# A low-rank update on one Trainium2 core: TensorE in a hardware loop, x narrowed to float16 before it is turned

## The chip, the core and the metric

The kernel runs on one core of a Trainium2 chip. Times are device microseconds of one execution; the time before is the median of three runs. One further execution was recorded by the hardware profiler, and the views shown here are of that one. Engines are called TensorE (PE; PEld is its weight load, PEldq the queue in front of that), VectorE (DVE), ScalarE (ACT), GpSimd (POOL) and SyncE (SP); a q behind a name is that engine's instruction queue, from which DMAs are issued too.

## What is computed

```python
batch, seq, d_model, r = 16, 512, 768, 16
def reference(x, A, B, scale):        # all float32, scale = 0.5
    lora = np.matmul(np.matmul(x, A), B)
    return (x + scale * lora).astype(np.float32)
```

x is 8192 tokens by 768, 25.2 MB in and as much out. A is 768 x 16 and B 16 x 768. The arithmetic is small; x has to come in, be multiplied twice through a width of 16, be added to the product, and go out.

## The kernel before

The 8192 tokens are 64 subtiles of 128 tokens. They are loaded in six parts of 2, 6, 8, 16, 16 and 16 subtiles (PARTS, line 13), each one DMA, all issued by SyncE (line 68, the last at line 96). All of x stays in SBUF: the result is written over it and stored from there (line 155), by SyncE too, in eight pieces of 2, 6, 8, 16 and then four times 8 subtiles. A and B come in through ScalarE's queue (lines 79, 80) into room that the last part of x takes later, so the last load waits until VectorE has turned and cast them into a_mm and b_mm (lines 87 to 93).

The work goes by chunks of up to four subtiles, 17 in all. For each chunk (the loop at line 157):

- `transposed` (line 109): for each of the six blocks of 128 columns, TensorE turns the chunk's subtiles, in float32, into a bank of PSUM (xt_ps, three buffers; line 113), and ScalarE copies the bank to SBUF as float16 (xt_sb, six buffers; line 115).
- `projected` (line 118): six matmuls with A as weights add up the 16 x 512 projection ps_yt (line 122); VectorE scales it to float16, yt_sb, two buffers (line 127).
- `added` (line 133): for each subtile two matmuls (512 and 256 columns) expand the projection into lora_ps, two buffers (line 139); VectorE adds that to x in place (line 145).
- `finished` (line 147): where a piece is complete, SyncE stores it.

The order on TensorE is written out: three blocks of chunk c turned, half of the previous chunk expanded, three more blocks turned, the other half expanded, then chunk c projected. Every instruction is unrolled. Semaphores are set by the framework from the tiles and their buffers; waits ride on the instruction that needs them.

Of the kernel before, what the change touches and what calls it, by code (L numbers as in the profile page):

```python
# [1 line left out]

# [6 lines left out]


MM_DT = mybir.dt.float16

PARTS = [2, 6, 8, 16, 16, 16]

STORES = {4: [8, 8], 5: [8, 8]}

CHUNK = 4


@with_exitstack  # L20
def kernel(
    ctx: ExitStack,
    tc: tile.TileContext,
    x: bass.AP,
    A: bass.AP,
    B: bass.AP,
    scale: bass.AP,
    out: bass.AP,
):

    nc = tc.nc
    fp32 = mybir.dt.float32
    P = 128

    x2 = x.flatten_outer_dims()
    out2 = out.flatten_outer_dims()
    T, D = x2.shape
    R = A.shape[1]  # L40
    ND = D // P
    assert D % P == 0 and sum(PARTS) * P == T
    n_splits = [(n0, min(512, D - n0)) for n0 in range(0, D, 512)]
    sc = float(scale)

    const = ctx.enter_context(tc.tile_pool(name="const", bufs=1))
    xpool = ctx.enter_context(tc.tile_pool(name="xp", bufs=1))
    xtpool = ctx.enter_context(tc.tile_pool(name="xtp", bufs=6))
    ypool = ctx.enter_context(tc.tile_pool(name="yp", bufs=2))
    ps_xt = ctx.enter_context(tc.tile_pool(name="ps_xt", bufs=3, space=bass.MemoryType.PSUM))  # L50
    ps_y = ctx.enter_context(tc.tile_pool(name="ps_y", bufs=1, space=bass.MemoryType.PSUM))
    ps_l = ctx.enter_context(tc.tile_pool(name="ps_l", bufs=2, space=bass.MemoryType.PSUM))


    parts = []
    tok = 0
    for i, S in enumerate(PARTS):
        parts.append([None, tok, S])
        tok += S * P

    def rows(t2, i):
        _, tok0, S = parts[i]
        return t2[ds(tok0, S * P), :].rearrange("(p s) d -> p s d", s=S)

    def loaded(i):
        S = parts[i][2]
        parts[i][0] = xpool.tile([P, S, D], fp32, name=f"x_sb{i}")
        nc.sync.dma_start(out=parts[i][0], in_=rows(x2, i))  # L68


    last = len(parts) - 1
    lastpool = ctx.enter_context(tc.tile_pool(name="lastp", bufs=1))
    room = lastpool.tile([P, parts[last][2], D], fp32, name="room", tag="last")
    NB = D // 32
    a_rows = room[0:32, 0, 0 : 32 * R].rearrange("b (a r) -> b a r", r=R)
    a_t = room[0:32, 1, 0 : 32 * R].rearrange("a (r b) -> a r b", r=R)
    b_f32 = room[0:R, 2, :]
    nc.gpsimd.memset(a_rows, 0.0)  # L78
    nc.scalar.dma_start(out=a_rows[0:NB, :, :], in_=A.rearrange("(b a) r -> b a r", a=32))
    nc.scalar.dma_start(out=b_f32, in_=B)  # L80
    loaded(0)
    loaded(1)
    for i in range(2, last):
        loaded(i)


    nc.vector.transpose(out=a_t, in_=a_rows.rearrange("b a r -> b r a"))  # L87
    a_mm = const.tile([P, ND, R], MM_DT, name="a_mm")
    a_tv = a_t[:, :, 0:NB].rearrange("a r (c k) -> a k c r", k=4)
    for k in range(4):  # L90
        nc.vector.tensor_copy(out=a_mm[ds(32 * k, 32), :, :], in_=a_tv[:, k, :, :])  # L91
    b_mm = const.tile([R, D], MM_DT, name="b_mm")
    nc.vector.tensor_copy(out=b_mm, in_=b_f32)  # L93

    parts[last][0] = lastpool.tile([P, parts[last][2], D], fp32, name="x_last", tag="last")
    nc.sync.dma_start(out=parts[last][0], in_=rows(x2, last))

    ident = const.tile([P, P], fp32, name="ident")
    make_identity(nc, ident)


    chunks = [
        (i, s0, min(CHUNK, S - s0))
        for i, (_, _, S) in enumerate(parts)
        for s0 in range(0, S, CHUNK)
    ]
    state = {}

    def transposed(c, j):
        i, s0, n = chunks[c]  # L110
        xt_ps = ps_xt.tile([P, CHUNK, P], fp32, name="xt_ps")
        for s in range(n):
            nc.tensor.transpose(xt_ps[:, s, :], parts[i][0][:, s0 + s, ds(j * P, P)], ident)  # L113
        xt_sb = xtpool.tile([P, CHUNK * P], MM_DT, name="xt_sb")
        nc.scalar.copy(out=xt_sb[:, 0 : n * P], in_=xt_ps[:, 0:n, :])  # L115
        state[c, j] = xt_sb

    def projected(c):
        n = chunks[c][2] * P
        ps_yt = ps_y.tile([R, CHUNK * P], fp32, name="ps_yt")  # L120
        for j in range(ND):
            nc.tensor.matmul(  # L122
                ps_yt[:, 0:n], a_mm[:, j, :], state.pop((c, j))[:, 0:n],
                start=(j == 0), stop=(j == ND - 1),
            )
        yt_sb = ypool.tile([R, CHUNK * P], MM_DT, name="yt_sb")
        nc.vector.tensor_scalar(  # L127
            out=yt_sb[:, 0:n], in0=ps_yt[:, 0:n], scalar1=sc, scalar2=None,
            op0=mybir.AluOpType.mult,
        )  # L130
        state[c] = yt_sb

    def added(c, subs):
        i, s0, n = chunks[c]
        subs = [s for s in subs if s < n]
        lora = {s: ps_l.tile([P, D], fp32, name="lora_ps") for s in subs}
        for s in subs:
            for n0, w in n_splits:
                nc.tensor.matmul(  # L139
                    lora[s][:, ds(n0, w)], state[c][:, ds(s * P, P)], b_mm[:, ds(n0, w)],  # L140
                    start=True, stop=True,
                )
        for s in subs:
            xs = parts[i][0][:, s0 + s, :]
            nc.vector.tensor_tensor(out=xs, in0=xs, in1=lora[s], op=mybir.AluOpType.add)  # L145

    def finished(c):
        i, s0, n = chunks[c]
        del state[c]
        end = 0  # L150
        for w in STORES.get(i, [parts[i][2]]):
            end += w
            if end == s0 + n:
                piece = slice(end - w, end)
                nc.sync.dma_start(out=rows(out2, i)[:, piece, :], in_=parts[i][0][:, piece, :])

    for c in range(len(chunks)):
        for j in range(3):
            transposed(c, j)
        if c >= 1:  # L160
            added(c - 1, (0, 1))
        for j in range(3, ND):
            transposed(c, j)
        if c >= 1:
            added(c - 1, (2, 3))
            finished(c - 1)
        projected(c)
    c = len(chunks) - 1
    added(c, (0, 1))
    added(c, (2, 3))  # L170
    finished(c)


# [1 line left out]
_INS = ['x', 'A', 'B', 'scale']  # L175
_OUTS = [((16, 512, 768), 'float32')]

_NUMBERS = {'scale': 0.5}


# [26 lines left out]
```

## Time and profile before

| | |
|---|---|
| time, median of 3 runs | 125.14 us (125.05 to 125.24) |
| the profiled execution | 124.9 us, of which the profile's span is 123.1 us |
| TensorE busy, in 614 matmuls | 97.8 us, 79% of the span |
| TensorE's weight loads | 60.8 us, 49% |
| VectorE busy | 70.3 us, 57% |
| ScalarE busy | 52.5 us, 43% |
| DMA, the queue of SyncE | 50.33 MB, 95.6% of 16 engines' span |
| DMA, instruction fetches (two queues) | 8 packets, 0.10 MB, 0.3% |
| mean rate of all DMA | 410 GB/s |
| chain that ended last | PE 71%, DMA 8%, VectorE 7% |

The span runs from the first instruction of the kernel to its last; the time holds 1.8 us more. A row of the page's groups reads: line, engine, operation, output <- input with shapes, count | busy us, mean ns of one | idle us of the engine just ahead of them and what ended it. A matmul's duration reaches from its start until its result is out, so consecutive ones overlap: their distance is less than the mean of one. The chain of waits follows the work back from the end: each piece started when the one above it was done.

### The profile page before, as it was taken

How to read it: one execution, taken by the hardware profiler on the slowest of the kernel's cores; microseconds unless marked ns; L12 is line 12 of the kernel's file. 1: busy time of each engine (PE TensorE's matmuls, PEld its weight loads, DVE VectorE, ACT ScalarE, POOL GpSimd, SP SyncE). 2: the span in 40 equal slices, each digit the busy share in tenths (PEclk: the TensorE clock that was granted, in tenths of full speed). 3: DMA queues.
4: the chain of work that ended last, by engine and by line, in shares of the span. 5: the costliest groups of instructions: out<-in, count | busy, mean ns of one | idle time of the engine just before them, and what ended most of it. 6: DMA issues, size and time to landing. Idle time of an engine off the chain costs nothing.

```text
span 123.1 us, 1615 instructions
## 1 busy us (share of the span) xinstructions
PE 97.8 (79%) x614; PEld 60.8 (49%) x614; DVE 70.3 (57%) x87; ACT 52.5 (43%) x103; POOL 1.1 (1%) x7
## 2 busy tenths in 40 slices
PE   0095999999949999999999999999999999530000
PEld 0083765657328566656657474757565666100000
DVE  0261056755884276868686868685767768880000
ACT  3060556455406573645555564737373736000000
POOL 3000000000000000000000000000000000000000
PEclk9999999999999999999999999999999999995555
DMA  2999998999799699799799999989979999999981
GB/s 61 406 431 427 471 519 367 415 500 431 335 511 479 290 511 468 319 479 495 295 411 462 444 407 495 479 351 479 452 311 463 415 439 426 421 447 439 415 383 64
DMA packets 2092, 50.54 MB, mean 410 GB/s; under 512 B 252, under 2 KB 252, under 8 KB 548
## 3 DMA queue, kind: packets, MB, share of 16 engines
q1 hardware_dynamic: 2016, 50.33, 95.6%
q10 hardware_dynamic: 68, 0.10, 0.4%
q8 instruction: 5, 0.08, 0.3%
q14 instruction: 3, 0.02, 0.0%
HBM read 25.26 MB, written 25.17 MB: 410 GB/s over the span
## 4 chain that ended last, share of the span: by engine, by line
PE 71%; DMA 8%; DVE 7%; issue 1%; DVEq 1%; SPq 0%; ACT 0%; ACTq 0%
PE xt_ps L113 38%; PE lora_ps L139 18%; PE ps_yt L122 15%; DMA x_sb<-in_x_dram 8%; DVE x_last L145 3%; DVE x_sb L145 3%; DVE yt_sb L127 1%; DVEq L202 1%; SPq L68 0%; ACT xt_sb L115 0%; ACTq L115 0%
## 5 line engine op out<-in xcount | busy, mean ns | idle before, releaser
L115 ACT CAST xt_sb<-xt_ps 128x512 f16<-128x512 f32 (+1 forms) x102 | 51.2, 569 | 49.9 <-PE xt_ps L113 49.6
L145 DVE TENSOR_TENSOR x_sb<-x_sb,lora_ps 128x768 f32<-128x768 f32 x48 | 43.5, 950 | 21.2 <-PE lora_ps L139 21.2
L113 PE MATMUL xt_ps<-ident,x_sb 128*128 128x128 f32 x288 | 39.7, 290 | 7.7 <-DMA x_sb<-in_x_dram 7.6
L113 PEld LDWEIGHTS xt_ps<-ident,x_sb 128*128 128x128 f32 x288 | 33.1, 147 | 16.7 <-issue 11.5
L139 PE MATMUL lora_ps<-b_mm,yt_sb 16*128 16x512 f16 (+1 forms) x128 | 26.8, 324 | 3.8 <-DVE yt_sb L127 1.6
L122 PE MATMUL ps_yt<-xt_sb,a_mm 128*16 128x512 f16 (+1 forms) x102 | 24.4, 375 | 0.0
L145 DVE TENSOR_TENSOR x_last<-x_last,lora_ps 128x768 f32<-128x768 f32 x16 | 14.5, 950 | 5.3 <-PE lora_ps L139 5.3
L139 PEld LDWEIGHTS <-yt_sb 16*128 16x128 f16 x128 | 9.5, 92 | 15.3 <-issue 8.3
L127 DVE TENSOR_SCALAR yt_sb<-ps_yt 16x512 f16<-16x512 f32 (+1 forms) x17 | 10.9, 642 | 7.9 <-PE ps_yt L122 7.9
L122 PEld LDWEIGHTS <-a_mm 128*16 128x16 f16 x102 | 7.9, 91 | 13.0 <-issue 5.1
L113 PE MATMUL xt_ps<-ident,x_last 128*128 128x128 f32 x96 | 12.2, 277 | 0.0
L113 PEld LDWEIGHTS xt_ps<-ident,x_last 128*128 128x128 f32 x96 | 10.3, 140 | 3.0 <-PE ps_yt L122 1.7
L93 DVE CAST b_mm<-room 16x768 f16<-16x768 f32 x1 | 0.5, 548 | 4.4 <-DMA room<-in_B_dram 4.4
L115 ACT ACT_TABLE_LOAD x1 | 1.3, 1283 | 1.9 <-POOL ident masks.py:199 1.9
L87 DVE STREAM_TRANSPOSE room<-room 32x512 f32<-32x512 f32 x1 | 1.0, 1031 | 1.1 <-DMA room<-in_A_dram 1.1
L91 DVE CAST a_mm<-room 32x96 f16<-32x96 f32 x4 | 0.9, 232 | 0.1
L78 POOL MEMSET room<- 32x512 f32 x1 | 0.5, 515 | 0.3 <-POOLq L188 0.3
masks.py:199 POOL TENSOR_SCALAR_AFFINE_SELECT ident<-ident 128x128 f32<-128x128 f32 x1 | 0.3, 292 | 0.1
masks.py:197 POOL MEMSET ident<- 128x128 f32 x1 | 0.2, 194 | 0.0
L188 POOL MEMSET const-bfloat16-1.0<- 128x1 bf16 x1 | 0.1, 101 | 0.0
L188 POOL MEMSET const-uint8-127<- 128x1 uint8 x1 | 0.1, 101 | 0.0
L188 POOL MEMSET const-float32-0.0<- 128x1 f32 x1 | 0.1, 98 | 0.2 <-issue 0.2
(1 smaller groups left out, 0.1 us busy)
## 6 DMA issues: line engine op xcount, KB each, us to landing
x_sb<-in_x_dram SPq DMA_DIRECT2D x2, 6144.0 KB, 39.7
out_dram<-x_sb SPq DMA_DIRECT2D x3, 3072.0 KB, 21.6
x_last<-in_x_dram SPq DMA_DIRECT2D x1, 6144.0 KB, 56.0
out_dram<-x_sb SPq DMA_DIRECT2D x1, 6144.0 KB, 28.2
out_dram<-x_last SPq DMA_DIRECT2D x2, 3072.0 KB, 13.5
x_sb<-in_x_dram SPq DMA_DIRECT2D x1, 3072.0 KB, 17.3
x_sb<-in_x_dram SPq DMA_DIRECT2D x1, 2304.0 KB, 10.5
out_dram<-x_sb SPq DMA_DIRECT2D x1, 2304.0 KB, 44.6
```

The source lines that it names most:

```text
L78: nc.gpsimd.memset(a_rows, 0.0)
L87: nc.vector.transpose(out=a_t, in_=a_rows.rearrange("b a r -> b r a"))
L91: nc.vector.tensor_copy(out=a_mm[ds(32 * k, 32), :, :], in_=a_tv[:, k, :, :])
L93: nc.vector.tensor_copy(out=b_mm, in_=b_f32)
L113: nc.tensor.transpose(xt_ps[:, s, :], parts[i][0][:, s0 + s, ds(j * P, P)], ident)
L115: nc.scalar.copy(out=xt_sb[:, 0 : n * P], in_=xt_ps[:, 0:n, :])
L122: nc.tensor.matmul(ps_yt[:, 0:n], a_mm[:, j, :], state.pop((c, j))[:, 0:n], start=(j == 0), stop=(j == ND - 1),)
L127: nc.vector.tensor_scalar(out=yt_sb[:, 0:n], in0=ps_yt[:, 0:n], scalar1=sc, scalar2=None, op0=mybir.AluOpType.mult,)
L139: nc.tensor.matmul(lora[s][:, ds(n0, w)], state[c][:, ds(s * P, P)], b_mm[:, ds(n0, w)], start=True, stop=True,)
L145: nc.vector.tensor_tensor(out=xs, in0=xs, in1=lora[s], op=mybir.AluOpType.add)
L188: nc = _bacc.Bacc("TRN2", target_bir_lowering=False, num_devices=1)
L202: with _tile.TileContext(nc) as tc:
```

## The change

The kernel body is rewritten with semaphores set by hand; the framework's scheduling of tiles is used for memory only.

- Parts are now 4, 4, 8, 16, 16 and 16 subtiles, stored in pieces of 4, 4, 8, 16 and four times 8. There are 16 chunks of four subtiles.
- x is not turned as float32. It is first narrowed to float16, by pieces of 4 subtiles x 256 columns, into three fixed buffers xh0, xh1 (by VectorE) and xh2 (by ScalarE). TensorE turns these, eight 128 x 128 blocks to a group, into float16 in three PSUM buffers xt_ps0 to 2; ScalarE copies each to xt0 to 2.
- The scaling of the projection goes from VectorE to ScalarE, into one buffer yt. There are two buffers lo_ps for the expanded subtiles, as before.
- A and B are loaded by SyncE, behind the first part of x, and GpSimd makes the identity as float16.
- TensorE runs chunks 1 to 15 as a hardware loop (`nc.Fori`). A loop's instruction can't wait for a rising count, so each of its waits is for one, and takes one off again (`taken`); the unrolled engines wait for rising counts.

The order on each engine is written out:

```diff
+LOADS = [4, 4, 8, 16, 16, 16]
+STORES = [4, 4, 8, 16, 8, 8, 8, 8]
...
+        load(0)
+        nc.sync.wait_ge(S["zeroed"], 1)
+        nc.sync.dma_start(
+            out=a_rows[0:NB, :, :], in_=A.rearrange("(b a) r -> b a r", a=32)
+        ).then_inc(S["a"], 16)
+        nc.sync.dma_start(out=b_f32, in_=B).then_inc(S["b"], 16)
+        for i in range(1, len(LOADS) - 1):
+            load(i)
+        nc.sync.wait_ge(S["prep"], 1)
+        load(len(LOADS) - 1)
...
+        narrowed(nc.scalar, 0, 2)
+        for c in range(NC):
+            for u in range(NU):
+                nc.scalar.wait_ge(S["turned"], NU * c + u + 1)
+                nc.scalar.copy(out=xt[u], in_=xt_ps[u]).then_inc(S[f"got{u}"], 1)
+            if c + 1 < NC:
+                narrowed(nc.scalar, c + 1, 2)
+            nc.scalar.wait_ge(S["proj"], c + 1)
+            nc.scalar.activation(
+                out=yt, in_=yt_ps, func=mybir.ActivationFunctionType.Copy, scale=sc
+            ).then_inc(S["y"], 1)
...
+        def summed(k):
+            nc.vector.wait_ge(S["lora"], k + 1)
+            nc.vector.tensor_tensor(
+                out=xs[:, k, :], in0=xs[:, k, :], in1=lo_ps[k % 2], op=add
+            ).then_inc(S["freed"], 1)
+            if k + 1 in ends:
+                nc.vector.drain().then_inc(S["added"], 1)
...
+        for c in range(NC):
+            for u in range(2):
+                if c + 1 < NC:
+                    nc.vector.wait_ge(S["turned"], NU * c + u + 1)
+                    narrowed(nc.vector, c + 1, u)
+                if c >= 1:
+                    for s in range(2 * u, 2 * u + 2):
+                        summed((c - 1) * CHUNK + s)
+        for s in range(CHUNK):
+            summed((NC - 1) * CHUNK + s)
...
+        def taken(name):
+            nc.tensor.wait_ge(S[name], 1).then_inc(S[name], -1)
+
+        def turned(u):
+            taken(f"fed{u}")
+            for j in range(2):
+                for s in range(CHUNK):
+                    i = nc.tensor.transpose(
+                        xt_ps[u][:, j, ds(s * P, P)], xh[u][:, s, ds(j * P, P)], ident
+                    )
+            i.then_inc(S["turned"], 1)
+
+        def projected(u):
+            taken(f"got{u}")
+            for j in range(2):
+                i = nc.tensor.matmul(
+                    yt_ps, a_mm[:, 2 * u + j, :], xt[u][:, j, :],
+                    start=(u == 0 and j == 0), stop=(u == NU - 1 and j == 1),
+                )
+            if u == NU - 1:
+                i.then_inc(S["proj"], 1)
+
+        def expanded(s):
+            if s == 0:
+                taken("y")
+            taken("freed")
             for n0, w in n_splits:
+                i = nc.tensor.matmul(
+                    lo_ps[s % 2][:, ds(n0, w)], yt[:, ds(s * P, P)], b_mm[:, ds(n0, w)],
                     start=True, stop=True,
                 )
+            i.then_inc(S["lora"], 1)
...
+        with nc.Fori(1, NC, engines=(mybir.EngineType.PE,)):
+            turned(0)
+            expanded(0)
+            expanded(1)
+            turned(1)
+            projected(0)
+            expanded(2)
+            expanded(3)
+            turned(2)
+            projected(1)
+            projected(2)
+        for s in range(CHUNK):
+            expanded(s)
```

In the loop, turned and projected are of chunk c, expanded of chunk c - 1. `narrowed(engine, c, u)` casts columns 256 u to 256 u + 255 of chunk c into xh[u]; each engine waits for a part of x once, at the first chunk of that part. prep is counted up when VectorE has made a_mm and b_mm. SyncE issues the stores in order, each behind a wait for added.

## The prediction

> **What bounds the kernel now.** I read the DMA first, then the chain that ended last, then the rows that price one chunk (four subtiles of 128 tokens). The DMA by stretches (length of the stretch, busy time of five engines with counts, granted clock, mean busy share of the 16 DMA engines, GB/s):
>
> ```profile
> 2.00:64.00 62.00, 54.44 (x337) 34.60 (x338) 35.58 (x46) 30.43 (x61) 0.00 (x0) 1.00 1.00 424
> 64.00:122.00 58.00, 43.34 (x279) 26.22 (x276) 34.73 (x42) 21.89 (x42) 0.00 (x0) 0.90 0.98 418
> ```
>
> The share is 1.00 while x is loaded (the last load lands at 8.2 + 56.0 = 64.2) and 0.98 while the result is stored. All loads and stores go through SP's queue in order, so no store moves before the last load is through. From then on the kernel is a full pipe of stores, as long as each is issued before the one ahead of it is done. The chain of waits nevertheless names TensorE (start us, us, what):
>
> ```profile
> 57.67 1.39 PE ps_yt L122 x6
> 59.06 1.46 PE xt_ps L113 x12
> 60.52 0.75 PE lora_ps L139 x4
> 61.27 1.46 PE xt_ps L113 x12
> 62.73 0.75 PE lora_ps L139 x4
> 63.48 1.39 PE ps_yt L122 x6
> ```
>
> A chunk takes TensorE 1.39 + 2 x 1.46 + 2 x 0.75 = 5.81 us without a gap; the last add ends at 110.4 and the last store is issued at 110.5. So two limits lie almost on each other. By the tile's own view:
>
> ```profile
> DMA to landing us min/median/max: 11.8/15.1/56.0
> ```
>
> The next to last store is issued at 99.9 and lands at 115.0, the last lands at 110.5 + 11.8 = 122.3, 7.3 us behind it. 3.146 MB at 0.43 MB/us are 7.3 us: the queue had no hole. How late could the last issue be? The first load (0.786 MB) took 5.4 us on an empty queue, 1.85 of it transfer at 425 GB/s, so some 3.55 us are fixed; a 3.146 MB store on an empty queue would take 7.4 + 3.55 = 10.95 us. It took 11.8: **slack 0.85 us**, last issue by about 111.35. A faster TensorE can gain next to nothing, since the store pipe is full; a later last add costs its delay, less 0.85 us.
>
> **The change, part by part.** The rows (line, engine, operation, shapes, count, busy us, mean ns, idle before):
>
> ```profile
> L115 ACT CAST xt_sb<-xt_ps 128x512 f16<-128x512 f32 x90 | 47.0, 595 | 44.0 <-PE xt_ps L113 44.0
> L115 ACT CAST xt_sb<-xt_ps 128x256 f16<-128x256 f32 x12 | 4.2, 375 | 5.9 <-PE xt_ps L113 5.6
> L139 PEld LDWEIGHTS <-yt_sb 16*128 16x128 f16 x128 | 9.5, 92 | 15.3 <-issue 8.3 <-DVE yt_sb L127 2.6
> L93 DVE CAST b_mm<-room 16x768 f16<-16x768 f32 x1 | 0.5, 548 | 4.4 <-DMA room<-in_B_dram 4.4
> L113 PEldq EVENT_SEMAPHORE  x4: 51/51/51, 6.1 to 81.0; - x4
> ```
>
> - Loads and stores move the same bytes in the same order; the first 32 subtiles still arrive as four loads, so load 3 should still land at about 2.2 + 32.9 = 35.1. A and B now stand behind load 0 on SP's queue (0.1 MB, 0.2 us). SP's wait for prep before the last load holds only that load and the stores; prep needs some 4 us of VectorE after load 0 lands near 8, so about 12 against the 8.2 of before, with loads queued until 49.6. Nothing lost.
> - Narrowing by VectorE (new, two per chunk, 128x1024): between the b_mm row (768 columns, 548 ns) and the a_mm row (96 columns, 232 ns) a column costs 0.47 ns, so 0.67 us; at the 1 column per 1.04 ns of the 16x512 row from PSUM (673 ns) 1.2 us. I take 0.67, as b_mm is the nearest SBUF row. VectorE per chunk: 2 x 0.67 + 4 x 0.9 = 4.9 us, no bound.
> - ScalarE: three copies 128x1024, one narrowing, one yt. From 256 to 512 columns the row grows by 220 ns, so 1024 columns cost 595 + 440 = 1.03 us. Nothing shows a ScalarE read from SBUF or of float16: 0.6 to 1.5 us, I take 1.03 for both. Back to back it saves 0.1 (six in 3.03 us). ScalarE per chunk 4 x 0.93 + 0.6 = 4.3 us, no bound either.
> - Transposes in float16, eight to a group: float32 ones follow every 121 ns. Float16 projections stream 512 columns in 232 ns, 58 ns for 128 columns, and a float16 weight load has 92 ns against 140. Between 58 and 121 I take 75 ns: 7 x 75 + 235 for the last to come out = 0.76 us. TensorE per chunk: 24 x 0.075 + 1.39 + 1.5 = 4.7 us, plus eleven semaphore instructions of 51 ns, 5.3 us. Below 5.81: by busy time everything gets faster.
> - **The ring of waits** is what I believe decides. lo_ps has two buffers, each waited for by name; yt and the three xh, xt_ps and xt have one each, and TensorE's order is fixed: turned(2) stands behind expanded(3), which needs the first two adds of the previous chunk. Hand-overs cost 0.05 us (VectorE's yt ends 34.34, TensorE starts 34.39). From one copy of xt2 to the next: copy 1.03; narrowing xh2, queued ahead of yt on ScalarE, 0.93; yt 0.50; hand-over and two waits 0.15, expanded(0) 0.48 to its end, hand-over 0.05; two adds 1.82; hand-over, wait and expanded(3) issued 0.05 + 0.05 + 0.375; wait and turned(2) 0.05 + 0.76; hand-over 0.05. **Sum 6.30 us a chunk**, with no engine above 5.3. (Second path to the first add: projection, back edge, turned(0), VectorE's narrowing: about equal.) Low end 5.85 (58 ns transposes, waits free), high end 7.1 (121 ns transposes, 1.5 us narrowing).
>
> The back edge of the loop is nowhere in this trace. The nearest rows are a semaphore instruction, 51 ns, and the smallest load, 3.7 us to landing, should code have to come from memory. I take 0.15 us; about 0.35 us a chunk hides beside ScalarE's narrowing. The Trainium skill (Advanced Engine Details and Errata, Control Flow Timing) gives about 108 ns for compare-and-branch, and its page Runtime: NRT & Kernel Launch, Instruction fetch mechanics, speaks against the change: a taken branch to a target outside the fetched window waits for a DMA. By the first the sum stays; the second would be the third rival; no run here shows either.
>
> **The sum.** VectorE's narrowing for chunk 4 waits for load 3, with chunk 2's adds queued behind it. 35.1 + 0.05 + 0.67 + 1.82 = 37.65; expanded(3), turned(2), copy: + 2.36 = 40.0 (xt2 of chunk 3). Twelve more chunks: + 75.6 = 115.6. Chunk 15: projection 0.70, yt 0.65, expanded 0.63, four adds 3.60 = 121.2; issue 0.15, store on an empty queue 10.95, end 0.8 (122.3 to 123.1 now): span 133.1.
>
> To that the clock. It shows in the same twelve transposes, early and later:
>
> ```profile
> 11.76 2.79 PE L113 MATMUL xt_ps<-ident,x_sb 128*128 128x128 f32 x12 [1.34 <-DMA x_sb<-in_x_dram]
> 15.36 1.53 PE L113 MATMUL xt_ps<-ident,x_sb 128*128 128x128 f32 x12
> ```
>
> Up to 14.8 us TensorE ran at half speed, and at 110.4 the granted clock fell again, after a stretch in which it was busy 1.18 of 3.41 us. With load 3 awaited it will stand still for some 4 us before 37, so a slow stretch behind that is likely: 0 to 3 us, I take 1.0. The Trainium skill (TensorE: Matmul & The Clock Gate, Part 4) says that transposes do not count as activity for the clock; the stretch from 11.76 to 14.8, nearly all transposes, raised it, so here the measurement decides. By the rule the sum would be that of the second rival.
>
> Span 134.1. The profiled execution took 124.9 for its span of 123.1, so + 1.8: **135.9**. (The median of 125.14 is 0.2 above that execution; I leave that out.)
>
> **The rivals.**
> - The ring is shorter: ScalarE and TensorE handle 16-bit data at twice the rate of their float32 rows (copy and narrowing -0.8 together). It decides below (111.35 - 0.15 - 5.58 - 40.0) / 12 = 5.47 us a chunk: then the last store is in time and the pipe of stores ends as now. For it: only float32 sources are in the rows. Against: ScalarE's rate a column is the same in every row. Time: 124.9 less a part of the 0.3% that instruction fetches take now, 124.6.
> - Clock: gaps keep TensorE at half speed. By the two rows above it is then 1.82 times as slow, 4.7 us become 8.6, with the semaphore instructions 9.1 a chunk: 12 x 2.8 more, about 170. Against: stretches busy 2.37 of 3.41 us held the full clock.
> - The back edge fetches code: 3.7 - 0.35 us times 15, up to 186; with a stall of 1 us, 146. Against: the loop's body is some 50 instructions.
>
> **How the numbers follow.** Forecast 0.72, with its own range from 129 (5.85 a chunk: 5.4 less, clock 1 less) to 147 (7.1: 9.6 more, clock 2 more). Shorter ring 0.15, clock 0.08, back edge 0.05. Range 125 to 147: it leaves out most of the shorter ring and the two slow cases' upper part. A measurement tells about 0.2% from no change. Faster 0.11 and same 0.04 are the shorter ring, slower 0.85 the rest.
>
> **What would show it.** Last store issued near 121, DMA share falling below 0.9 after 64 us; chunks 6.3 us apart; TensorE waiting for yt and for VectorE's adds; turned groups of 0.76 us; VectorE's narrowing 0.67, ScalarE's 1.0. Wrong if chunks are under 5.5 us apart, or TensorE's idle time sits at the loop's edge, or the granted clock stays at 0.5.

## The result and the profile after

The changed kernel takes 139.64 us (median of six runs, 137.83 to 141.4) against 125.12 us: **1.110 times as long, 95% interval 1.103 to 1.117**. The prediction was 135.9 us, range 125 to 147. The profiled execution took 141.0 us, its span is 139.2 us. (Ratios and intervals, here and in the experiments, leave out runs more than 1.5% above the fastest of their kernel, here those of 141.0 and 141.4 us, while medians and ranges hold all; why the runs differ so much, TensorE's clock, is a finding below.)

TensorE, granted clock and DMA of the changed kernel, in 40 slices of its span:

```profile
PE   0058509999969699969699999986999998964000
PEclk9999965555899955999955959599959686868555
DMA  4999999999889999989999999999259505950792
```

The clock of the kernel before rose once and stayed at full speed to the end of its work. Here it swings between full and half all the way. The DMA begins to run out of stores after some 70% of the span. By stretches (TensorE, its weight loads, VectorE, ScalarE, GpSimd; clock, DMA share, GB/s):

```profile
2.00:64.00 62.00, 45.10 (x280) 20.22 (x280) 35.67 (x49) 33.36 (x39) 0.12 (x1) 0.81 1.00 422
64.00:122.00 58.00, 52.04 (x319) 21.85 (x318) 40.26 (x50) 37.05 (x42) 0.00 (x0) 0.78 0.82 350
```

Loading is as before: share 1.00. Storing has fallen from 0.98 to 0.82, since the stores are late. The end of VectorE's work, and the stores' times from issue to landing (shortest, median, longest):

```profile
125.58 3.63 DVE L144 TENSOR_TENSOR xs<-xs,lo_ps 128x768 f32<-128x768 f32 x4 [3.40 <-PE lo_ps L202]
```

```profile
DMA to landing us min/median/max: 8.7/15.1/42.9
```

The last add ends at 129.2 instead of 110.4, and the last store, issued at 129.3 and alone in the queue, needs 8.7 us. One chunk at full clock, from one copy of xt2 to the next (start us, us, engine, line, operation):

```profile
59.73 1.01 ACT L133 COPY xt<-xt_ps 128x1024 f16<-128x1024 f16 x1 [1.32 <-PE xt_ps L182]
60.64 1.05 ACT L91 CAST xh<-xs 128x1024 f16<-128x1024 f32 x1
...
60.89 0.59 PE L190 MATMUL yt_ps<-xt,a_mm 128*16 128x512 f16 x2 [0.66 <-PEq L176]
...
61.44 0.61 PE L182 MATMUL xt_ps<-ident,xh 128*128 128x128 f16 x8
61.59 0.58 ACT L137 ACTIVATE yt<-yt_ps 16x512 f16<-16x512 f32 x1
...
62.47 0.81 PE L202 MATMUL lo_ps<-b_mm,yt 16*128 16x512 f16 x4 [0.42 <-PEq L176]
62.98 1.82 DVE L144 TENSOR_TENSOR xs<-xs,lo_ps 128x768 f32<-128x768 f32 x2 [0.20 <-PE lo_ps L202]
...
64.95 0.48 PE L202 MATMUL lo_ps<-b_mm,yt 16*128 16x512 f16 x2 [0.17 <-PEq L176]
...
65.36 0.62 PE L182 MATMUL xt_ps<-ident,xh 128*128 128x128 f16 x8
...
66.02 1.01 ACT L133 COPY xt<-xt_ps 128x1024 f16<-128x1024 f16 x1 [1.15 <-PE xt_ps L182]
```

That is the ring of waits, step for step: copy, narrowing, yt, expanded(0), two adds, expanded(3), turned(2), copy. (The other way to yt, copy and projected(2), ends at 60.89 + 0.59 = 61.48, just ahead of the narrowing's 61.69, so the narrowing itself adds little.) It closes in 66.02 - 59.73 = 6.29 us; predicted were 6.30. Over the whole run it is slower: the yt of chunk 3 starts at 40.94, that of chunk 15 at 124.18, 6.94 us a chunk. The theory is that the difference is the clock.

### The profile page after: what moved, and what is told of

It reads as the page before. It is cut to its first block, busy times and chain, and to the rows that moved or that the text cites. A ratio compares the mean times of both kernels' runs of the same rounds, so it can differ in the third digit from the quotient of the medians.

```text
span 139.2 us, 1699 instructions
## 1 busy us (share of the span) xinstructions
PE 101.0 (73%) x608; PEld 42.7 (31%) x608; DVE 79.7 (57%) x102; ACT 73.1 (52%) x81; POOL 1.2 (1%) x7
## 5 line engine op out<-in xcount | busy, mean ns | idle before, releaser
L133 ACT COPY xt<-xt_ps 128x1024 f16<-128x1024 f16 x48 | 48.4, 1012 | 41.8 <-PE xt_ps L182 41.8
L144 DVE TENSOR_TENSOR xs<-xs,lo_ps 128x768 f32<-128x768 f32 x64 | 58.1, 948 | 9.0 <-PE lo_ps L202 8.9
L93 DVE CAST xh<-xs 128x1024 f16<-128x1024 f32 x32 | 21.9, 690 | 40.4 <-PE xt_ps L182 26.4
L182 PE MATMUL xt_ps<-ident,xh 128*128 128x128 f16 x384 | 37.6, 258 | 8.5 <-PEq L176 8.5
L190 PE MATMUL yt_ps<-xt,a_mm 128*16 128x512 f16 x96 | 38.1, 491 | 6.1 <-PEq L176 5.7
L202 PE MATMUL lo_ps<-b_mm,yt 16*128 16x512 f16 (+1 forms) x128 | 31.4, 352 | 12.6 <-PEq L176 12.3
L182 PEld LDWEIGHTS xt_ps<-ident,xh 128*128 128x128 f16 x384 | 28.2, 116 | 29.8 <-issue 29.8
L91 ACT CAST xh<-xs 128x1024 f16<-128x1024 f32 x16 | 16.8, 1048 | 5.5 <-DMA xs<-in_x_dram 5.5
L202 PEld LDWEIGHTS lo_ps<-b_mm,yt 16*128 16x128 f16 x128 | 9.3, 96 | 32.5 <-issue 30.3
L137 ACT ACTIVATE yt<-yt_ps 16x512 f16<-16x512 f32 x16 | 9.4, 585 | 3.4 <-PE yt_ps L190 3.4
```

Of the source, the lines that this page charges most:

```text
L91: i = engine.copy(out=xh[u], in_=src)
L93: i = engine.tensor_copy(out=xh[u], in_=src)
L133: nc.scalar.copy(out=xt[u], in_=xt_ps[u]).then_inc(S[f"got{u}"], 1)
L137: nc.scalar.activation(out=yt, in_=yt_ps, func=mybir.ActivationFunctionType.Copy, scale=sc).then_inc(S["y"], 1)
L144: nc.vector.tensor_tensor(out=xs[:, k, :], in0=xs[:, k, :], in1=lo_ps[k % 2], op=add).then_inc(S["freed"], 1)
L182: i = nc.tensor.transpose(xt_ps[u][:, j, ds(s * P, P)], xh[u][:, s, ds(j * P, P)], ident)
```

## The experiments

The theory after the result: two things add up, the ring (6.29 us a chunk) and a clock that falls to half because TensorE has pauses. The rivals: the loop's back edge or its counted waits; the narrowing itself; and that stores are no floor at all. The kernel before took 124.9 to 125.0 us beside every experiment.

| run | what | us (runs) | ratio to before, 95% | chunk at full clock | mean clock |
|---|---|---|---|---|---|
| e1_unrolled | loop written out | 141.13 (139.8 to 141.9) | 1.126 (1.116 to 1.136) | 6.28 | 0.80 |
| e2_early_turn | turned(2) ahead of expanded(2), projected(1) ahead of expanded(3) | 125.91 (six at 125.6 to 126.9, two at 144.6 and 147.4) | 1.006 (1.004 to 1.008) | 5.27 | 0.82 |
| e3_filler | transposes in the pauses | 134.33 (133.3 to 136.7) | 1.072 (1.064 to 1.079) | 6.33 | 0.91 |
| e5_early_turn_filler | both, 10 transposes a chunk | 126.66 (126.5 to 129.9) | 1.012 (1.009 to 1.015) | 5.60 | 0.91 |
| e6_rising | unrolled, rising counts | 132.25 (129.5 to 133.3) | no interval | 5.98 | 0.87 |
| e7_before_float16 | before, narrowing alone | 125.94 (six at 124.8 to 126.2, two at 133.7 and 133.9) | 1.004 (1.001 to 1.007) | | 0.83 |
| e8_before_two_blocks | before, less work | 128.44 (128.0 to 129.4) | 1.029 (1.026 to 1.033) | | 0.66 |
| e10_early_turn_rising | e2 and e6, A and B over ScalarE's queue | two at 125.5 and 125.6, four at 145.3 to 149.7 | 1.005 (1.004 to 1.007), of the two | 5.04 (8.64 at half) | 0.64 |
| e11_rows128 | expansions over 128 rows | 129.90 (129.8 to 130.2) | 1.040 (1.038 to 1.041) | 6.19 | 0.95 |
| e12_early_turn_rows128 | e10 over 128 rows | 125.42 (125.2 to 126.4) | 1.005 (1.002 to 1.007) | 4.88 | 0.88 |
| e13_two_blocks_rows128 | e8 over 128 rows | 124.91 (124.4 to 125.2) | 0.999 (0.998 to 1.000) | | 0.79 |
| e14_loop_early_turn_rows128 | the change with both mends | 125.53 (125.5 to 125.8) | 1.005 (1.004 to 1.006) | 5.11 | 0.88 |

The chunk is the distance between ScalarE's yt of one chunk and of the next; the clock is the mean over the profiled run's span, its idle end included and the time ahead of the first record taken as full.

**Is it the loop's back edge?** e1_unrolled:

```diff
-        with nc.Fori(1, NC, engines=(mybir.EngineType.PE,)):
+        for _ in range(1, NC):
```

> TensorE's loop is written out by Python 15 times; its waits, which take one off again, stay as they are, so only the back edge goes (and more instructions are fetched). Ring of waits: from one copy of xt2 to the next 6.29 us at full clock, with the edge hidden beside ScalarE's narrowing, so chunks stay 6.29 us apart at full clock and the time stays within 2% of the changed kernel's 139.6 us. Back edge as the cause: each of 15 edges costs 0.5 us or more, chunks fall below 5.8 us and the time below 132 us.

141.13 us: no gain, and chunks 6.28 us apart at full clock in both. The back edge is not the cause; what it costs is hidden, as the sum had it.

**Is it the ring?** e2_early_turn:

```diff
             projected(0)
+            turned(2)
             expanded(2)
-            expanded(3)
-            turned(2)
             projected(1)
+            expanded(3)
             projected(2)
```

> One move in TensorE's order: turned(2) goes ahead of expanded(2), and projected(1) between expanded(2) and expanded(3). Ring of waits: the two adds drop out of the ring; copy of xt2, narrowing, yt, expanded(0) and (1), turned(1), projected(0), turned(2) give about 5.3 us a chunk at full clock, so the last add comes near 104 to 113 (by how often the clock falls) and the time is 125 to 130 us. Clock alone as the cause: the same matmuls and pauses a chunk, so the time stays at 136 to 140 us. Back edge: no change either.

125.91 us with the same instructions: moving one group of transposes (and one of the projections behind it) ahead of a wait for adds takes 13.7 us off. Chunks are 5.27 us apart at full clock (expected 5.3), and the DMA share while x is stored, 0.82 in the changed kernel, is 0.98 from 57 to 110 us:

```profile
57.00:110.00 53.00, 49.30 (x382) 21.57 (x380) 48.93 (x59) 44.20 (x50) 0.00 (x0) 1.00 0.98 421
```

But two of eight runs took 145 to 147 us, with a mean clock of 0.66 to 0.68, which the ring does not explain.

**Is it the clock?** e3_filler puts 19 transposes of the identity a chunk where TensorE waits (shown here); e5_early_turn_filler has the early turn too, and 10 a chunk:

```diff
+        def filler(u, m):
+            for _ in range(m):
+                nc.tensor.transpose(xt_ps[u][:, 0, 0:P], ident, ident)
...
             turned(0)
+            filler(2, 6)
             expanded(0)
...
             expanded(2)
+            filler(2, 3)
             expanded(3)
             turned(2)
             projected(1)
+            filler(0, 10)
             projected(2)
```

> TensorE turns the identity 19 more times a chunk, into a PSUM buffer that is free then, where it would wait: 6 ahead of the wait for yt, 3 ahead of expanded(3), 10 ahead of projected(2); their results are overwritten and read by nobody. Ring and clock: the pauses are filled, the granted clock stays at 1.0 from about 35 us on, all chunks are 6.3 to 6.5 us apart, the last add comes near 115 to 118 and the time is 125.5 to 129 us. If the clock's swings do not matter: 6 to 10% more work on TensorE, 139 us or more.

134.33 us: 285 more transposes make the kernel 5.3 us faster. From 45 us on the clock is full and chunks are 6.33 us apart, as expected:

```profile
50.00:119.00 69.00, 68.33 (x625) 36.10 (x624) 52.08 (x64) 47.70 (x55) 0.00 (x0) 1.00 0.88 379
```

The expected time was too low: it counted twelve chunks from 34.5 us, where the changed kernel has the yt of chunk 2, not of chunk 3, and the clock was at half again from 38 to 45 us.

> The move of the early turn and the fillers (6 ahead of the wait for yt, 4 ahead of projected(2)) together. Ring and clock: chunks 5.3 to 5.6 us apart at full clock, the last add before 108, the queue of stores never runs dry and the time is that of the pipe of loads and stores, 124.5 to 125.5 us, no better than before. If the stores are not the floor it would be below 122 us.

126.66 us, a little above what was expected. The last add ends at 110.3 (expected before 108), the last store is issued at 110.4 as in the kernel before, and the span is 124.4 us; besides, this kernel's runs take 2.0 to 2.3 us outside their span instead of 1.8. Why is open.

**Are the counted waits a cost?** e6_rising, written out as e1 is:

```diff
-            nc.tensor.wait_ge(S[name], 1).then_inc(S[name], -1)
+            count[name] = count.get(name, 0) + 1
+            nc.tensor.wait_ge(S[name], count[name])
```

> TensorE written out as in e1, and each of its waits is for a rising count and takes nothing off, as on the other engines; the order is that of the changed kernel. Ring of waits: what the counted waits cost in the ring goes, at most the 0.30 us from the end of yt to expanded(0) and the 0.15 us from an add to expanded(3) down to about 0.05 each; 5.9 to 6.1 us a chunk at full clock, and with the clock falling as before 134 to 138 us. Counted waits as the main cause: below 5.5 us a chunk and below 130 us.

Each counted wait is an instruction of its own on TensorE's queue. In the changed kernel's trace (shortest, median, longest in ns; then who waited for them, us in total, times):

```profile
L176 PEldq EVENT_SEMAPHORE  x176: 51/51/903, 8.4 to 127.4; - x176
...
  PE lo_ps L202: 12.3, 24
  PE xt_ps L182: 8.5, 1
  PE yt_ps L190: 5.7, 15
```

In e6 the waits ride on the matmuls again. ScalarE's yt and the expansion behind it:

```profile
62.54 0.58 ACT L137 ACTIVATE yt<-yt_ps 16x512 f16<-16x512 f32 x1
...
63.17 0.82 PE L205 MATMUL lo_ps<-b_mm,yt 16*128 16x512 f16 x4 [0.27 <-ACT yt L137]
```

63.17 - (62.54 + 0.58) = 0.05 us, where the changed kernel has 62.47 - (61.59 + 0.58) = 0.30. The chunk is 5.98 us, within the expected 5.9 to 6.1; so the counted waits cost 0.3 us a chunk. The time is 132.25 us, lower than the expected 134 to 138; the clock also fell less often (0.87 on the mean). So they are a real part of the ring, not its main part.

**Is it the narrowing?** e7_before_float16 is the kernel before with x narrowed by VectorE and ScalarE and turned in groups of eight, and yt scaled by ScalarE into one buffer; framework and unrolling are as before, and TensorE's order as near to it as three groups allow:

```diff
-        for j in range(3):
-            transposed(c, j)
+        for u in range(2):
+            transposed(c, u)
         if c >= 1:
             added(c - 1, (0, 1))
-        for j in range(3, ND):
-            transposed(c, j)
+        transposed(c, 2)
```

> The kernel before, its framework, its unrolled TensorE and its semaphores, with one part of the change: x is narrowed to float16 by VectorE and ScalarE, turned from there in groups of eight, and yt is scaled by ScalarE (one buffer). TensorE turns two groups, expands (0, 1) of the chunk before, turns the third, expands (2, 3), projects. Ring: here the third turn does not wait for adds, so chunks of about 5.3 to 5.8 us and 125 to 127 us. If narrowing itself is the cause (its work on VectorE and ScalarE, or the pauses it puts into TensorE): 132 us or more.

125.94 us: the narrowing costs nothing that shows. Two of eight runs took 133.7 and 133.9 us, at a mean clock of 0.78.

**Do loads and stores set the floor?** e8_before_two_blocks leaves out four of six column blocks (the projection is of 256 columns only):

```diff
-        for j in range(3):
+        for j in range(1):
             transposed(c, j)
...
-        for j in range(3, ND):
+        for j in range(1, 2):
             transposed(c, j)
```

> The kernel before with four of the six blocks of 128 columns left out: not turned, not copied and not multiplied with A (so the projection is of 256 of 768 columns). TensorE's chunk falls from 5.81 to some 3 us. Pipe of loads and stores as the floor: the time stays within 0.5 us of 125.0. TensorE as the bound of the kernel before: below 115 us.

128.44 us: less work, and slower than with all of it. Its clock:

```profile
PEclk9999999999655798555555555555555555555555
```

(The page shows full speed up to the first record of the clock, 29 us here; the durations of the transposes, four in 1.1 us, show half before it.) So "less work" and "lower clock" were mixed, and the floor was not tested. e10_early_turn_rising made the same point more sharply:

> The early turn of e2, the unrolled TensorE with rising counts of e6, and A and B loaded over ScalarE's queue as in the kernel before. Ring: about 5.0 us a chunk, VectorE's own work, at full clock; the last store is in time and the time is the pipe's, 124.8 to 125.4 us, that of the kernel before. If the setting up of the changed kernel costs on its own: 125.6 to 126 us.

Two runs at 125.5 us as expected, four at 145 to 150. TensorE and its clock in one of the four:

```profile
PE   0059649999999999999999999999999999994000
PEclk9999975555555555555555555555555799999555
```

By one stretch of it:

```profile
24.00:112.00 88.00, 88.00 (x391) 33.86 (x391) 50.78 (x62) 46.71 (x52) 0.00 (x0) 0.50 0.83 358
```

TensorE is busy without a gap for 88 us and is kept at half speed. So it is not pauses as such. What differs between stretches after which the clock rose and others? It changes at multiples of 3.41 us. Two such stretches of the changed kernel, all of TensorE first, then the expansions (line 202) alone:

```profile
49.19:52.60 3.41, 3.41 (x19) 1.39 (x16) 3.13 (x5) 1.01 (x1) 0.00 (x0) 0.50 0.83 360
52.60:56.01 3.41, 3.17 (x15) 1.03 (x14) 0.54 (x1) 2.54 (x3) 0.00 (x0) 0.50 1.03 447
```

```profile
49.19:52.60 3.41, 1.46 (x4) 0.42 (x4) 0.50 0.83 360
52.60:56.01 3.41, 0.00 (x0) 0.02 (x1) 0.50 1.03 447
```

The first is full and the clock stayed at half; the second is less full and it rose. The first holds 1.46 us of expansions, matmuls over 16 rows; the second none. I took this over all such stretches of eight runs (before, after, e1, e2, e6, e7, e8, e10), as the share in which transposes and projections, over 128 rows, are busy (the two added up). At half clock: behind none below 0.78 did it rise, behind all from 0.87 up it did, between these both happened. At full clock: it fell behind all up to 0.42, behind none from 0.55 up. So a theory that can be tried: **only matmuls over 128 rows count as activity for the clock**. e11_rows128 gives the expansions 128 rows, 112 of them zeros; their columns stay, and so nearly does their time (0.38 us for 512 columns at full clock, 0.37 before):

```diff
-    b_mm = sb.tile([R, D], MM_DT, name="b_mm")
+    b_mm = sb.tile([P, D], MM_DT, name="b_mm")
...
-    yt = sb.tile([R, CHUNK * P], MM_DT, name="yt")
+    yt = sb.tile([P, CHUNK * P], MM_DT, name="yt")
...
+        nc.gpsimd.memset(b_mm, 0.0).then_inc(S["zeroed"], 1)
+        nc.gpsimd.memset(yt, 0.0).then_inc(S["zeroed"], 1)
```

> The changed kernel with one thing: yt and b_mm are given 128 rows, of which 16 hold values and 112 zeros, so the expansions are matmuls over 128 rows; same columns, same order, same waits. Clock theory (only matmuls over 128 rows count as activity for the clock; in the runs so far half clock rose behind every stretch of 3.41 us in which transposes and projections were busy for 0.87 or more of it and behind none below 0.78, however busy the expansions): the expansions now count, the clock stays at 1.0 once x flows, chunks are 6.29 us apart from yt of chunk 3 near 41 on, the last add near 121, time 130 to 133.5 us. If pauses of any kind lower the clock: no change, 138 to 141 us.

129.90 us, 9.7 us less than the changed kernel and just under the expected 130 to 133.5, and the runs now lie within 0.3%. Its clock, and its work between the yt of chunk 3 and the end:

```profile
PEclk9999996799999999999999999999999999999655
```

```profile
41.00:116.00 75.00, 57.27 (x442) 27.65 (x441) 56.91 (x71) 50.64 (x58) 0.00 (x0) 1.00 0.96 409
```

TensorE is busy 76% of the time, and the clock does not fall in this stretch: pauses like these do not lower it by themselves. The chunk is 6.19 us: what is left is the ring.

e12_early_turn_rows128 is e10 with the same edit:

> e10 (early turn, unrolled, rising counts, A and B over ScalarE's queue) with the 128 rows of e11. Clock theory: e10 was at 125.5 us in two runs and at 145 to 150 in four, because at half clock its expansions fill TensorE and the others never reach the share; with 128 rows all runs are at 125 to 125.6 us, chunks 5.04 us apart, the median falls by 22 us. If the rows do not count: half the runs or more stay above 140 us. A time below 124.7 would beat the kernel before.

125.42 us in the median of eight, against four of six at 145 to 150. Two of the eight lie above the expected 125 to 125.6, at 125.9 and 126.4. e13_two_blocks_rows128 repeats the test of the floor with the clock mended:

> e8 (the kernel before with four of six column blocks left out) with the 128 rows. e8 was slower than the kernel before because its clock stayed at half (0.656 on the mean). Clock theory and pipe of loads and stores: the clock stays at 1.0 for most of the work, the last add comes long before 105 us, and the time is that of the pipe, 124.5 to 125.3 us, with half of TensorE's work gone. If TensorE bounds the kernel before: below 118 us.

124.91 us. The stretch of stores, the last two stores' issue, and all stores' times to landing:

```profile
64.00:122.00 58.00, 23.41 (x99) 9.68 (x96) 28.71 (x34) 4.32 (x8) 0.00 (x0) 0.66 0.97 417
```

```profile
87.85 10.37 SPq L158 DMA_DIRECT2D out_dram<-x_last  x2
```

```profile
DMA to landing us min/median/max: 24.4/32.8/49.8
```

The last store is issued at 97.9, 12.6 us earlier than in the kernel before, and the span is the same 123.1 us: it waits in the queue instead. The floor is the pipe of loads and stores. (The clock is not full throughout here, and two stretches with a share of 0.92 and 0.96, zeros counted as rows and the three kinds added up, did not raise it. TensorE as a whole was busy for 0.86 and 0.85 of them; how the zero rows count in detail is open.)

e8 and e13 also hold the plainest pair of stretches for the theory. Both lie at half clock and are filled mostly by expansions, over 16 rows in e8 (first line) and over 128 in e13 (second line); the lines count the expansions alone (length, TensorE, its weight loads, clock, DMA):

```profile
53.21:56.63 3.42, 2.47 (x8) 0.67 (x6) 0.50 1.06 460
```

```profile
31.38:34.80 3.42, 2.95 (x8) 0.86 (x8) 0.50 1.07 460
```

In e8 TensorE had no pause at all in that stretch, and the clock stayed at half; in e13 it was busy for 0.86 of it, nearly all of that expansions, and the clock rose.

e14_loop_early_turn_rows128 is the changed kernel with its loop and counted waits and the two mends:

> The changed kernel with its hardware loop, its counted waits and its loads, and the two mends alone: the early turn of e2 and the 128 rows of e11. Ring and clock: chunks of 5.1 to 5.3 us, the clock at 1.0, the last store issued before 111, so the time is that of the pipe plus what the changed kernel's start and end take, 125.2 to 126.0 us, in every run (e2 had two of eight at 144 to 148). If the loop or the counted waits cost time beyond the ring: 128 us or more.

125.53 us, six runs within 0.3%. The hardware loop as such costs nothing that shows once ring and clock are mended. Neither it nor e12 beats the kernel before. e12's last store is issued at 103.5 and lands 18.7 us later, at 122.2, where the kernel before has 122.3; so TensorE has no part in the last 0.5%. e12's span then ends 1.3 us behind that landing, that of the kernel before 0.8. What takes the half microsecond at the end was not tried.

## Why the prediction was right, and where it was not

The direction, the size (1.110 measured, 1.088 forecast) and the range were right. The time was 3.7 us above the forecast: the clock's term was 8.7 too small and the other terms together some 5 too large. That these largely cancel is luck.

- **The floor** was read rightly: no store moves before the loads are through, and a faster TensorE gains next to nothing (e13).
- **The slack was mis-sized.** A store of 3.1 MB alone in the queue was put at 10.95 us; it takes 8.7. So the slack of the kernel before was 11.8 - 8.7 = 3.1 us, not 0.85, and the end of the sum 2.2 us too long. The fixed 3.55 us came from the very first load, behind which four more were issued before it landed; whether that made it slow was not tried.
- **Ring of waits, 6.30 us: right**, 6.29 measured. The pieces: narrowing by ScalarE 1.05 (taken 1.03), copies 1.01 (1.03), narrowing by VectorE 0.69 (0.67), eight transposes 0.62 (0.76, of which the 235 ns for the last one stood in no row; 56 ns apart, they leave 0.23 for it), yt's end to the expansion 0.30 (0.15). The last two offset each other, which is luck too. ScalarE's copy of float16 is no shorter than the float32 rows made it, so the 0.8 us that the first rival took off copy and narrowing was not there. The low end of 5.85 does not follow from its own terms: transposes of 58 ns take 0.12 off and four free waits 0.20, which leaves 5.98, what e6 measured with free waits. e2 shows that the ring, and not any engine's work, held the chunk above 5.3 us.
- **The back edge**, 0.15 us and hidden: right as far as it shows (e1, e14). The page cited against the change (Runtime: NRT & Kernel Launch, Instruction fetch mechanics) spoke of a taken branch that waits for a DMA; no such stall is in the trace: in the chunk shown, the last projection ends at 61.48 and the next round's transposes start at 61.44.
- **The mis-sized step is the clock**: "a slow stretch behind that is likely: 0 to 3 us, I take 1.0". Holding it (e11) takes 9.7 us off. The rival of half speed was put at 0.08 for the reason that "stretches busy 2.37 of 3.41 us held the full clock". In those stretches 0.43 of the time was matmuls over 128 rows, by this study's count just at the edge. I measured all of TensorE's busy time, where only a part seems to count. So the second rival came true for some 40% of the time (34 of the 83 us from the yt of chunk 3 to that of chunk 15). Its price was right: 8.6 us a chunk without the semaphore instructions, and 8.64 in e10, which has none.
- **The rule on transposes** (the Trainium skill, TensorE: Matmul & The Clock Gate, Part 4) was rightly set aside: e3's fillers are transposes alone, and with them the clock is full from 45 us on.
- **The sum in its parts.** With the clock held, the change costs 129.9 - 125.0 = 4.9 us: the ring beyond the floor; forecast without the clock term were 10.0. 2.2 of the 5.1 us between them are the store; 1.3 are twelve chunks of 6.19 instead of 6.30; the rest is the yt of chunk 3, at 38.85 in e11 instead of the 40.9 of the sum (2.1), less some 0.6 that the tail took more, most of it behind the last landing (1.3 us to the end of the span instead of 0.8). The clock brings 9.7 instead of 1.0. That yt of chunk 3 starts at 40.94 in the changed kernel, as the sum has it, is chance: there half clock had delayed it.

The trace of the kernel before would have allowed more. A stretch in which TensorE was busy for 0.72 (7.96 to 11.37 us) did not raise the clock (the transposes at 11.76 still ran at half speed), while one of 0.69 (35.26 to 38.68) held it: what holds the clock need not bring it back, so a pause can cost more than its own length.

## What to carry to other kernels

Where loads and stores fill the pipe, ask first when the last store must be issued; then follow one buffer's chain of waits around once, through every engine, since its sum is the chunk's time even when no engine is busy all of it. A group moved ahead of a wait that it does not need can be worth more than any faster instruction. And judge TensorE's clock by the stretches of the trace in which it rises and falls, by kind of matmul: work that is made shorter, or that runs over few rows, can lower the clock and cost more than it saved.

## What the runs showed of the hardware

- TensorE's clock changed at multiples of 3.41 us between full and half speed. Matmuls over 16 rows seemed not to hold it up, or to count for little (the runs don't tell these apart): TensorE was busy without a gap for 88 us at half clock (e10); the same columns over 128 rows, most of them zeros, kept it at full clock (e12, of the same order: 1.00 from 40 to 104.8 us; e11: 1.00 from 41 to 116). In the changed kernel it fell again and again although no pause of TensorE between 40 and 124 us was longer than 0.67 us.
- The state can keep itself: at half clock the expansions take a larger part of each stretch, so the other matmuls do not reach the share that raises it (in e10 0.84 at most, until one stretch of 0.90 raised the clock at 116 us). The same program then took 125.5 or 149.7 us (e10).
- A wait that takes a count off is an instruction of 51 ns on TensorE, and 0.30 us passed from the end of yt to the matmul behind two of them, against 0.05 where the wait rides on the matmul.
- Eight float16 transposes of 128 x 128 took 0.62 us at full clock, one every 56 ns; twelve float32 ones 1.53 us, one every 0.11 to 0.12 us.
